# Seven half-size products instead of eight in the first product of the second layer's MLP

## The chip, the cores and the metric

The kernel runs on one core of a Trainium2 chip. The metric is the device time of one execution in microseconds. The engines of the core are called here as in the profile: PE (TensorE, the matrix engine, with PEld for its weight loads), DVE (VectorE), ACT (ScalarE), POOL (GpSimd) and SP (SyncE, which issues the DMAs).

## What is computed

One inference step of a trunk of two layers over 128 context tokens and 512 latent tokens (640 in all), model width 1024. Layer 0 mixes tokens with gated and retention scans, layer 1 with latent attention. After each mixer comes the part that this change is about:

```
def sq_relu_mlp(h, w1, w2):
    u = jax.nn.relu(jnp.einsum('bld,df->blf', h, w1))       # 1024 -> 4096
    return jnp.einsum('blf,fd->bld', jnp.square(u), w2)     # 4096 -> 1024

hc = pre_norm_mod(xc, norm_mlp_pre[l], sh2c, sc2c)          # context tokens; hl: latent tokens
xc = post_norm_residual(xc, sq_relu_mlp(hc, w_mlp1[l], w_mlp2[l]), norm_mlp_post[l], gt2c)
```

The shifts, scales and gates (sh2c, sc2c, gt2c) come from a product of a condition vector with w_ada, here called the modulation.

## The kernel before

All data are float32. A float32 product is made by PE from float32r operands: each operand is split into a rounded high part and a low part (the rest), and `mm3` issues three matmuls: high by high, high by low, low by high.

**Who sets the order.** Nothing is issued in the order of the source text. The parts of the computation are generators; a planner (`Weave`) runs them against its own cost table for each engine, and issues an instruction when its model says that the engine and the operands are there. On DVE, threads of a lower priority number come first, and among equals the one born first. Each engine then executes its instructions in the order so found; semaphores keep the data right. Since one helper (line 269) records every instruction, the profile shows that line for nearly all of them, and the tiles' names tell them apart. Buffers are handed out by `Slots`: `take` waits until one is free, `drop` gives it back.

**Weights.** `weights` loads each unit (512 KB, 128 partitions x 1024 elements) into one of 3 raw buffers. `weight_rooms` then takes room for high and low part from 10 slots of 4 KB per partition (`wp`), in the order of the list of units, and `weight_split` makes the high part on ACT (`wh`, a cast) and the low part on DVE (`wl`, a subtraction); then the raw buffer is given back. A unit holds two of the ten slots.

**The MLP** (`mlp`, called for each layer). The hidden width of 4096 is cut into 8 blocks of 512. The tokens after the norm lie transposed in `hT[0]` (high) and `hT[1]` (low), 128 rows of the width x 5 token tiles x 8 chunks x 128 tokens. In each block:
- The first product (`mlp1`) makes the hidden columns in four slices of 128 (f = 0 to 3), each for two groups of token tiles (three tiles, 384 tokens, and two tiles, 256). One product sums over 8 chunks of the width, 24 matmuls; a slice has 48. It takes a PSUM bank (`p1`) from `psg`, which has 3.
- `relu` takes the bank: ACT makes relu into `r` and its square into `hid` (high part), POOL squares `r` in place, DVE subtracts to get the low part.
- The second product (`mlp2`): for both halves of the 1024 output columns and the five token tiles, 4 slices x 3 matmuls of 512 columns into a bank `p2`; `add` adds the bank to `y` in SBUF (ACT copies it in block 0). In the last block the order is token tile by token tile, and `tail` makes the gated norm, the residual with `x` and the output.

A block needs 8 weight units: four for the first product, then four for the second (two for each output half).

**The modulation.** `ada_half` and `ada_cols` compute one section of it on DVE from tiles `rada` (256 KB loads), at a lower priority than the rest. In the second layer's MLP this is the last section, whose gate `tail` needs at the end; it starts in block 0, when `running` is set. Its sums lie in two buffers of their own (`pada`). `tmp` is a set of 4 temporaries that also others take.

Of the kernel before, what the change touches and what calls it, by code (L numbers as in the profile page):

```python
# [11 lines left out]
F32 = mybir.dt.float32  # L12
F32R = mybir.dt.float32r
# [6 lines left out]
P = 128  # L20
# [311 lines left out]
class Trunk:  # L332
# [70 lines left out]
    def weight(self, src, shape, lo="vector", pair=False, quota=None, room=None, prio=1):  # L403
# [2 lines left out]
        self.wlist.append((src, shape, ev, lo, pair, quota, room, prio))  # L406
        return ev

    def weights(self):

        loads = [Event() for _ in self.wlist]
        self.w.spawn(self.weight_rooms(loads))
        for item, load in zip(self.wlist, loads):
            if isinstance(item, Event):
                continue
            src, shape = item[:2]
            raw, hr = yield from self.take(self.raw, [P] + shape, F32, "raw")
            parts = list(src(raw) if callable(src) else [(raw, src)])
            self.w.aside(lambda: [self.nc.sync.dma_start(a, b) for a, b in parts],
                         then=lambda at: self.w.set(load, (raw, hr, at)))  # L420
            yield

    def weight_rooms(self, loads):
        for item, load in zip(self.wlist, loads):
            if isinstance(item, Event):
                yield item
                continue
# [153 lines left out]
    def ada_half(self, l, sec, half, rest, n=KC):  # L581

        nc = self.nc
        acc = [self.pada.tile([P, 512], F32, tag=f"ada{c}", name=self.nm("ada")) for c in range(2)]
# [12 lines left out]
        return acc  # L597

    def ada_cols(self, l, sec, half, acc, res, room=None):

        nc = self.nc
        tr, ht = room or (yield from self.take(self.tmp, [P, 512], F32, "tr"))
# [5 lines left out]
        self.drop(ht)  # L608
        yield
        ps, hp = yield from self.take(self.psg if room else self.psum, [P, 512], F32, "pc")  # L610
# [14 lines left out]
    def ada(self, l, sec, ev, rest, free=None):  # L625


        nc = self.nc
        res = self.mod_tile(sec)
        for half in range(2):  # L630
            if (l, sec) in ADA_EVEN:
                yield from self.ada_tensor(l, sec, half, res)
                continue
            acc = yield from self.ada_half(l, sec, half, rest)
            yield from self.ada_cols(l, sec, half, acc, res)
# [12 lines left out]
        self.drop(hr)  # L648
        self.w.spawn(self.gate_rows(dram, ev, free))
# [210 lines left out]
    def mlp_units(self, l):  # L860
        w1 = self.io["w_mlp1"][l].rearrange("(k p) f -> p k f", p=P)
        w2 = self.io["w_mlp2"][l].rearrange("(f p) n -> p f n", p=P)
        res = []
        for b in range(FF // 512):
            lo = "vector"
            prio = 0 if b else 1
            u1 = [self.weight(w1[:, :, fc * P:(fc + 1) * P], [KC, P], lo, prio=prio) for fc in range(b * 4, b * 4 + 4)]
# [138 lines left out]

    def mlp(self, ph, l, ready, xs, gate, mods, gfree):
        nc, io, w = self.nc, self.io, self.w
        shid = self.slots(ph, f"hid{l}", 5)
        sr = self.slots(ph, f"relu{l}", 4)  # L1010
        NB = FF // 512
        self.pada = self.pool(ph, f"ada{l}", 1)
        self.ada_later(ADA_MLP if l == 0 else ADA_LAST, self.slots(ph, f"rada{l}", 4))
# [19 lines left out]
        def tail(t, ev):  # L1033

            c = 0 if t == 0 else 1
            y, sm = ys[t][0], sms[t][0]
            gr = yield gate
            for half in range(2):
                ps, hp = yield ev[half]
                s = slice(half * 512, half * 512 + 512)  # L1040
                nc.vector.tensor_add(y[:, s], y[:, s], ps)
                self.drop(hp)
                yield
                nc.scalar.activation(self.junk[:, 0:512], y[:, s], AF.Square, accum_out=sm[:, 4 + half:5 + half])
                yield
                nc.vector.tensor_mul(y[:, s], y[:, s], gr[c][:, s])
                yield
            if gfree:
                self.at_last(left, lambda: w.set(gfree))
            x = xs[t][0]  # L1050
            if mods is None:
                dst = io["y_prompt"][0] if t == 0 else io["y_sample"][0, (t - 1) * P:t * P, :]
                yield from self.residual(x, y, sm, dst)
            else:
                yield from self.residual(x, y, sm)
                yield from self.pre_norm(t, x, y, sm, mods, out_ready)
            self.drop(ys[t][1], sms[t][1])

        def add(ps, hp, t, half, b):
# [4 lines left out]
                nc.vector.tensor_add(yh, yh, ps)  # L1064
            self.drop(hp)
            yield

        for b in range(NB):
            u1, u2 = self.u_mlp[l][b]
# [25 lines left out]
            if b == 0:  # L1095
                order = [(f, 0) for f in range(4)] + [(f, 1) for f in range(4)]

            for f, g in order:
                yield from mlp1(f, g)

            def mlp2(half, t, ev=None):
                ps, hp = yield from self.take(self.psg, [P, 512], F32, "p2")
# [15 lines left out]
                    w.spawn(add(ps, hp, t, half, b))  # L1118

            if b == 0:  # L1120
                w.set(self.running[l])
# [13 lines left out]
        if mods:  # L1135
            yield self.mod[1, 4]
        return out_ready


    def rope(self, out, x, lt, t12, rtab):  # L1140
# [908 lines left out]
```

## Time and profile before

| | us |
|---|---|
| median of three runs | 1542.08 (1541.82 to 1544.7) |
| the profiled execution | 1542.66 |
| its span, first to last instruction | 1540.9 |
| PE busy in the span | 1495.1 (97%) |
| DVE busy | 962.6 (62%) |
| ACT busy | 636.6 (41%) |
| POOL busy | 165.4 (11%) |

The rows below come from the profiled execution. A matmul's duration in the trace overlaps its neighbours' durations, so the cost of one is the step from start to start in a stretch without gaps. In rows of the timeline, neighbouring instructions of one kind are merged, and x2 means two of them. The second layer's MLP runs from 1087 to the end, the first layer's from about 357 to 803.

### The profile page before, as it was taken

The page shows a single profiled execution, that of the slowest core. Times are in us where ns is not written, and L with a number is a line of the kernel's source. Part 1 is how long each engine was busy: PE and PEld are TensorE (multiplying, and loading weights), DVE is VectorE, ACT ScalarE, POOL GpSimd, SP SyncE. Part 2 cuts the span into 40 slices and gives each one's busy share as a digit, 9 for nine tenths or more (in the row PEclk, how much of TensorE's full clock was granted, in tenths as well). Part 3 has the DMA queues.
Part 4 walks back from the last instruction along what each step waited for, and adds up shares of the span by engine and source line. Part 5 has one row for each costly group of instructions (what it writes and reads, how often), then busy time and mean ns, then how long its engine had stood idle before and what let it go on. Part 6 is the DMA issues. An engine that isn't in the chain of part 4 may idle for free.

```text
span 1540.9 us, 22938 instructions
## 1 busy us (share of the span) xinstructions
PE 1495.1 (97%) x8731; PEld 1329.5 (86%) x8731; DVE 962.6 (62%) x1912; ACT 636.6 (41%) x1467; POOL 165.4 (11%) x181
## 2 busy tenths in 40 slices
PE   5999999999999999999997999999999999999997
PEld 2687888889899889889987899988989988998996
DVE  4464674766777877777778788886675333334336
ACT  3583533555423223223256476665532322322322
POOL 0000210001021012012100100000101201210210
PEclk8999999999999999999998999999999999999999
DMA  9546222233655444444325000032353222222211
GB/s 329 161 155 216 86 69 69 68 96 110 179 158 145 144 135 142 140 136 145 102 66 143 19 22 24 33 107 79 110 172 109 71 81 69 83 82 67 72 55 68
DMA packets 146733, 166.18 MB, mean 108 GB/s; under 512 B 11984, under 2 KB 92480, under 8 KB 146624
## 3 DMA queue, kind: packets, MB, share of 16 engines
q1 hardware_dynamic: 146624, 164.73, 35.1%
q8 instruction: 68, 1.11, 0.3%
q14 instruction: 41, 0.34, 0.1%
HBM read 158.73 MB, written 5.96 MB: 107 GB/s over the span
## 4 chain that ended last, share of the span: by engine, by line
PE 91%; DVE 4%; ACT 2%; DMA 2%; issue 1%; SPq 0%; DVEq 0%; ACTq 0%
PE p L269 56%; PE pg L269 19%; PE ps L269 13%; PE pqk L269 2%; DMA rada<-in_w_ada 1%; PE pv L269 1%; DVE y L269 1%; DVE sm L269 1%; ACT junk L269 1%; DVE x L269 1%; DMA raw<-in_w_in_even 0%; ACT h L269 0%; DVE rope L269 0%; ACT sm L269 0%; PE pc L269 0%
## 5 line engine op out<-in xcount | busy, mean ns | idle before, releaser
L269 PE MATMUL p<-hT,wh 128*128 128x256 f32 (+1 forms) x2048 | 446.7, 309 | 0.0
L269 PE MATMUL p<-wh,hid 128*128 128x512 f32 x1280 | 399.3, 390 | 0.0
L269 PEld LDWEIGHTS p<-hT,wh 128*128 128x128 f32 x2048 | 345.5, 189 | 1.3
L269 PE MATMUL p<-hT,wl 128*128 128x256 f32 (+1 forms) x1024 | 317.0, 310 | 0.0
L269 ACT CAST wh<-raw 128x1024 fp32r<-128x1024 f32 (+3 forms) x169 | 172.8, 1026 | 266.8 <-PE p L269 231.8
L269 PEld LDWEIGHTS p<-wh,hid 128*128 128x128 f32 x1280 | 240.2, 188 | 49.3
L269 DVE TENSOR_TENSOR wl<-raw,wh 128x1024 fp32r<-128x1024 f32 (+3 forms) x165 | 197.3, 1199 | 132.9 <-ACT wh L269 128.0
L269 PE MATMUL pg<-wh,hT 128*128 128x512 f32 (+3 forms) x840 | 264.7, 389 | 0.0
L269 PE MATMUL p<-wl,hid 128*128 128x512 f32 x640 | 249.6, 390 | 0.0
L269 POOL TENSOR_TENSOR r<-r 128x384 f32<-128x384 f32 (+1 forms) x128 | 133.0, 1039 | 1008.4 <-ACT hid L269 890.1
L269 PEld LDWEIGHTS p<-hT,wl 128*128 128x128 f32 x1024 | 193.9, 189 | 0.0
L269 PEld LDWEIGHTS pg<-wh,hT 128*128 128x128 f32 x840 | 155.0, 190 | 32.3 <-issue 9.2
L269 ACT ACTIVATE r<-p 128x384 f32<-128x384 f32 (+1 forms) x128 | 56.1, 438 | 269.8 <-PE p L269 269.8
L269 DVE TENSOR_TENSOR y<-y,p 128x512 f32<-128x512 f32 x140 | 95.9, 685 | 93.2 <-PE p L269 92.8
L269 DVE SCALAR_TENSOR_TENSOR ada<-rada,cT,ada 128x512 f32<-128x512 f32 x196 | 146.7, 782 | 0.0
L269 PE MATMUL pg<-wl,hT 128*128 128x512 f32 (+3 forms) x360 | 141.7, 394 | 0.0
L269 PEld LDWEIGHTS p<-wl,hid 128*128 128x128 f32 x640 | 120.2, 188 | 24.1
L269 DVE TENSOR_TENSOR hid<-r,hid 128x384 fp32r<-128x384 f32 (+1 forms) x128 | 62.5, 488 | 124.3 <-POOL r L269 124.2
L269 PEld LDWEIGHTS pg<-wl,hT 128*128 128x128 f32 x360 | 68.6, 191 | 11.9 <-issue 2.5
L269 ACT ACTIVATE hid<-r 128x384 fp32r<-128x384 f32 (+1 forms) x128 | 60.4, 472 | 2.3
L269 PE MATMUL ps<-kn,qn 128*128 128x320 f32 (+1 forms) x216 | 47.8, 311 | 0.9 <-DVE hT L269 0.4
L269 PE MATMUL ps<-pt,v 128*128 128x256 f32 (+1 forms) x264 | 43.5, 290 | 1.1 <-DVE pt L269 0.7
(255 smaller groups left out, 1777.1 us busy)
## 6 DMA issues: line engine op xcount, KB each, us to landing
raw<-in_w_mlp SPq DMA_DIRECT2D x128, 512.0 KB, 4.1
rada<-in_w_ada SPq DMA_DIRECT2D x160, 256.0 KB, 3.2
rada<-in_w_ada SPq DMA_DIRECT2D x16, 512.0 KB, 8.7
raw<-in_w_in_even SPq DMA_DIRECT2D x16, 512.0 KB, 4.7
x<-in_x_sample SPq DMA_DIRECT2D x8, 512.0 KB, 7.4
gate<-gate SPq DMA_DIRECT2D x8, 512.0 KB, 4.5
raw<-in_w_out_even SPq DMA_DIRECT2D x8, 512.0 KB, 4.9
raw<-in_w_out_odd SPq DMA_DIRECT2D x8, 512.0 KB, 3.8
```

The lines of the kernel that those rows point to most:

```text
L269: emit = lambda: real(*a, **k)
```

## The change

In blocks 2 to 7 of the second layer (`PLAIN` = 2), the first product of two slices of 128 hidden columns at once is made by the scheme of Strassen and Winograd. Rows (chunks 0 to 3 and 4 to 7 of the width), hidden columns (the two slices) and tokens (the two halves of 64 of every tile) are halved, and the 2 x 2 x 2 = 8 products of halves are replaced by 7 products of 4 chunks and 320 tokens, of which four use sums or differences of weight halves, and four use sums or differences of token halves. `combine` makes the four quarters of the result from the seven. The second product and its weights are as before.

- **Weights** (`weight_pair`, `pair_load`, `pair_rooms`): the two units of a pair are loaded into two raw buffers together. DVE makes four differences of 512 elements in `tmp`; seven high parts (ACT) and seven low parts (DVE) of 512 elements go to one slot each. The raw buffers are given back when all that read them are done.
- **Tokens** (`token_sums`): the three sums S0 to S2 are made once, from 3 additions and 3 more sums for each token tile, and split into high and low part. They need space: the `x` tiles of the residual are written to DRAM as soon as a tile's norm is done, and their five buffers hold most of the sums; a pool `sums` has the rest. S3 is made when block 1's first product has been issued, and overwrites the quarter of `hT` that is no longer read. Then also four PSUM banks pass from `psum` to `psg`, which has 7.
- **Results**: DVE takes the banks (`p7`), ACT the first; `square` makes relu and square in one DVE operation, the high part on ACT and the low part on DVE. POOL has no part in it.
- **The loop**: the fourteen products of a block, then the second product, of which the first four banks are begun with slices 0 and 1, and continued with 2 and 3 afterwards. In the last block `load_back` loads `x` again once its last first product is issued.
- **The modulation** starts at block 3 in place of 0, has two buffers for its loads in place of four, and its sums lie in two of the four `tmp`.

```
+    def pair_rooms(self, got, at, evs):
+        (r0, h0), (r1, h1) = got
+        b11, b21, b12, b22 = r0[:, 0:4], r0[:, 4:8], r1[:, 0:4], r1[:, 4:8]
...
+        go(0, b11, (yield from room()), seen)
+        go(1, b21, (yield from room()), seen)
+        r = yield from room()
+        t1, ht1 = yield from tmp()
+        t2, ht2 = yield from tmp()
+        nc.vector.tensor_sub(t1, b12, b11)
+        nc.vector.tensor_sub(t2, b22, t1)
+        yield
...
+        nc.vector.tensor_sub(t3, b22, b12)
...
+        nc.vector.tensor_sub(t4, b21, t2)
...
+        go(6, b22, (yield from room()), seen)
...
     def mlp(self, ph, l, ready, xs, gate, mods, gfree):
+        seven = l == 1
-        sr = self.slots(ph, f"relu{l}", 4)
+        sr = self.slots(ph, f"relu{l}", 7 if seven else 4)
-        self.pada = self.pool(ph, f"ada{l}", 1)
+        self.pada = None if seven else self.pool(ph, f"ada{l}", 1)
...
+            if seven:
+                xs[t] = yield xev[t]
...
+        def square(r, hr, h, half, ev):
+            s = slice(half * 64, half * 64 + 64)
+            rv = r.rearrange("p (t q) -> p t q", q=64)
+            nc.vector.scalar_tensor_tensor(r, r, 0.0, r, op0=ALU.max, op1=ALU.mult)
+            yield
+            nc.scalar.copy(h[:, 0, :, s], rv)
+            yield
+            nc.vector.tensor_sub(h[:, 1, :, s], rv, h[:, 0, :, s].bitcast(F32))
...
+        def products(units, hid, hev):
+            A = [[[self.hT[i][:, :, k + j, q:q + 64] for j in range(4)] for i in range(2)]
+                 for k, q in ((0, 0), (4, 0), (4, 64))]
...
+            for i, tok in enumerate((A[0], A[1], S[1], S[0], S[2], A[2], S[3])):
+                if i == 2:
+                    yield three
+                if i == 6:
+                    yield four
+                wh, wl, held = yield units[i]
+                ps, hp = yield from self.take(self.psg, [P, 512], F32, "p7")
+                for k in range(4):
+                    self.mm3(ps[:, 0:320], wh[:, k], wl[:, k], tok[0][k], tok[1][k], k == 0, k == 3)
+                self.drop(*held)
+                w.set(done[i], (ps[:, 0:320], hp))
+                yield "next"
...
+            if seven and b >= PLAIN:
+                if b == PLAIN + 1:
+                    w.set(self.running[l])
...
+                def begin(i):
+                    banks[i] = yield from self.take(self.psg, [P, 512], F32, "p2")
+                    yield from part2(*todo[i], (0, 1), banks[i][0])
+                pair = [products(u1[i], hid, hev) for i in range(2)]
+                for p in (0,) * 7 + (1,) * 7:
+                    yield from step(pair[p])
+                if last:
+                    self.drop(*xtokens)
+                    w.spawn(load_back())
...
+                for i, (half, t) in enumerate(todo):
+                    while len(banks) < min(len(todo), i + (4 if i == 0 else 1)):
+                        yield from begin(len(banks))
+                    yield from part2(half, t, (2, 3), ps)
...
+    def token_sums(self, S, rest, ready, xs, parked, tokens, sr, first_done, three, four):
+        for t in range(NT):
+            yield ready[t]
+            nc.sync.dma_start(parked[t], xs[t][0])
+            self.drop(xs[t][1])
...
+            nc.vector.tensor_add(a11, h(0, t, 0, 0), h(1, t, 0, 0))
+            nc.vector.tensor_add(a21, h(0, t, 0, 64), h(1, t, 0, 64))
+            nc.vector.tensor_add(s1, h(0, t, 4, 64), h(1, t, 4, 64))
+            nc.vector.tensor_add(s1, s1, a21)
+            nc.vector.tensor_sub(s2, s1, a11)
+            nc.vector.tensor_sub(a11, a11, a21)
...
+PLAIN = 2
```

`combine` has, for each pair, one ACT copy of a bank and seven DVE sums of 320 elements that read a bank, and four calls of `square`.

## Rows read from the trace of the kernel before

**Rows 1.** The page, busy time by engine and the chain by engine.

```profile
PE 1495.1 (97%) x8731; PEld 1329.5 (86%) x8731; DVE 962.6 (62%) x1912; ACT 636.6 (41%) x1467; POOL 165.4 (11%) x181
...
PE 91%; DVE 4%; ACT 2%; DMA 2%; issue 1%; SPq 0%; DVEq 0%; ACTq 0%
```

**Rows 2.** Chain in order of time, second MLP: start us, us, engine and tile.

```profile
1173.10 340.48 PE p L269 x1908
```

**Rows 3.** PE timeline, block 0 of that MLP: start us, us, operation, shape, count.

```profile
1095.70 0.51 PE L269 MATMUL p<-hT,wh 128*128 128x384 f32 x2
...
1100.38 0.51 PE L269 MATMUL p<-hT,wh 128*128 128x384 f32 x2
...
1105.45 0.40 PE L269 MATMUL p<-hT,wh 128*128 128x256 f32 x2
...
1116.96 0.40 PE L269 MATMUL p<-wh,hid 128*128 128x512 f32 x1
...
1118.12 0.62 PE L269 MATMUL p<-wh,hid 128*128 128x512 f32 x2
...
1131.04 0.62 PE L269 MATMUL p<-wh,hid 128*128 128x512 f32 x2
```

**Rows 4.** The same, first matmul of the second product in block 2.

```profile
1228.32 0.40 PE L269 MATMUL p<-wh,hid 128*128 128x512 f32 x1
```

**Rows 5.** PE timeline, second layer's input projection: 320 columns.

```profile
854.01 1.92 PE L269 MATMUL pg<-wh,hT 128*128 128x320 f32 x12
855.77 0.90 PE L269 MATMUL pg<-wp,hT 128*128 128x320 f32 x5
```

**Rows 6.** Busy us by engine, granted clock, DMA: blocks 0 and 3 (second MLP).

```profile
1087.00:1144.00 57.00, 57.00 (x329) 52.19 (x328) 38.56 (x70) 28.38 (x60) 6.71 (x8) 1.00 0.42 125
...
1255.00:1310.60 55.60, 55.60 (x315) 50.87 (x314) 20.16 (x26) 15.05 (x25) 8.66 (x8) 1.00 0.26 76
```

**Rows 7.** The same view, a block of the first layer's MLP.

```profile
526.20:581.60 55.40, 55.40 (x315) 50.55 (x314) 43.84 (x66) 15.43 (x33) 8.65 (x8) 1.00 0.49 143
```

**Rows 8.** DVE groups by form: count, busy us, mean ns (ada: second MLP alone).

```profile
L269 DVE TENSOR_TENSOR wl<-raw,wh 128x1024 fp32r<-128x1024 f32 x153 | 186.8, 1223 | 122.9 <-ACT wh L269 122.6
...
L269 DVE TENSOR_TENSOR y<-y,p 128x512 f32<-128x512 f32 x140 | 95.9, 685 | 93.2 <-PE p L269 92.8
...
L269 DVE TENSOR_TENSOR hid<-r,hid 128x384 fp32r<-128x384 f32 x64 | 35.7, 557 | 100.8 <-POOL r L269 100.8
...
L269 DVE TENSOR_TENSOR hid<-r,hid 128x256 fp32r<-128x256 f32 x64 | 26.8, 419 | 23.5 <-POOL r L269 23.5
...
L269 DVE TENSOR_TENSOR wp<-raw,wp 128x512 fp32r<-128x512 f32 x16 | 10.9, 685 | 1.8 <-ACT wp L269 1.6
...
L269 DVE SCALAR_TENSOR_TENSOR ql<-pg,sm,qpe 128x256 f32<-128x256 f32 x5 | 2.4, 482 | 0.1
...
L269 DVE SCALAR_TENSOR_TENSOR ada<-rada,cT,ada 128x512 f32<-128x512 f32 x28 | 20.7, 781 | 0.0
```

**Rows 9.** ACT group by form: the cast of half a weight.

```profile
L269 ACT CAST wp<-raw 128x512 fp32r<-128x512 f32 x16 | 9.9, 624 | 1.8 <-PE p L269 1.8
```

**Rows 10.** MLP weight loads (KB, median us to landing); landings between 1187 and 1320.

```profile
raw<-in_w_mlp SPq DMA_DIRECT2D x128, 512.0 KB, 4.1
...
DMA to landing us min/median/max: 4.0/4.1/5.1
```

**Rows 11.** Busy us by engine and granted clock, end of the first MLP.

```profile
810.00:815.00 5.00, 1.40 (x12) 1.18 (x11) 4.63 (x12) 4.14 (x14) 0.00 (x0) 1.00 0.22 42
...
815.00:820.00 5.00, 2.18 (x9) 1.89 (x9) 5.00 (x15) 2.23 (x7) 0.00 (x0) 0.50 0.78 273
```

**Rows 12.** The end: busy by window, PE's last matmul, the chain's last residual.

```profile
1520.00:1525.00 5.00, 5.00 (x24) 4.14 (x23) 4.08 (x9) 1.59 (x6) 0.00 (x0) 1.00 0.28 105
...
1532.22 0.39 PE L269 MATMUL p<-wh,hid 128*128 128x512 f32 x1
...
1536.58 0.75 DVE x L269
```

**Rows 13.** DMA issues: `x` written to DRAM in the attention, KB, us to landing.

```profile
park<-x SPq DMA_DIRECT2D x5, 512.0 KB, 4.1
```

More of the change, by code (lines that the diff above doesn't have):

```diff
@@ L407, in weight, with weight_pair, pair_load, done @@
         return ev
+    def weight_pair(self, w1, fc):
+        evs = [Event() for _ in range(7)]
+        self.wlist.append((w1, fc, evs))
+        return evs
+    def pair_load(self, w1, fc, load):
+        got = []
+        for i in range(2):
+            got.append((yield from self.take(self.raw, [P, KC, P], F32, "raw")))
+        at = [0.0]
+        left = [2]
+        def done(t):
+            at[0] = max(at[0], t)
+            left[0] -= 1
+            if not left[0]:
+                self.w.set(load, (got, at[0]))
+        for i in range(2):
+            self.w.aside(lambda i=i: self.nc.sync.dma_start(got[i][0], w1[:, :, (fc + i) * P:(fc + i + 1) * P]), then=done)
+            yield
@@ L414, in weights @@
             if isinstance(item, Event):
+                continue
+            if len(item) == 3:
+                yield from self.pair_load(item[0], item[1], load)
                 continue
@@ L426, in weight_rooms @@
                 yield item
+                continue
+            if len(item) == 3:
+                got, at = yield load
+                yield from self.pair_rooms(got, at, item[2])
                 continue
@@ L583, in ada_half @@
         nc = self.nc
-        acc = [self.pada.tile([P, 512], F32, tag=f"ada{c}", name=self.nm("ada")) for c in range(2)]
+        acc, held2 = [], []
+        for c in range(2):
+            if self.pada:
+                acc.append(self.pada.tile([P, 512], F32, tag=f"ada{c}", name=self.nm("ada")))
+            else:
+                a, ha = yield from self.take(self.tmp, [P, 512], F32, "ada")
+                acc.append(a)
+                held2.append(ha)
         for kc in range(n):
@@ L596, in ada_half, with ada_cols @@
             yield rest
-        return acc
-    def ada_cols(self, l, sec, half, acc, res, room=None):
+        return acc, held2
+    def ada_cols(self, l, sec, half, acc, held, res):
         nc = self.nc
-        tr, ht = room or (yield from self.take(self.tmp, [P, 512], F32, "tr"))
+        tr, ht = yield from self.take(self.tmp, [P, 512], F32, "tr")
         sm, hs = yield from self.take(self.rows, [P, 2, 16], F32, "sums")
@@ L607, in ada_cols @@
             yield
-        self.drop(ht)
+        self.drop(ht, *held)
         yield
-        ps, hp = yield from self.take(self.psg if room else self.psum, [P, 512], F32, "pc")
+        ps, hp = yield from self.bank()
         nc.tensor.matmul(ps[:, 0:32], self.fold, sm.rearrange("p c b -> p (c b)"), start=True, stop=True)
@@ new lines, in combine @@
+        def combine(done, first, second):
+            (ha, ea), (hb, eb) = first, second
+            keep = lambda: self.take(sr, [P, 320], F32, "c")
+            p, hp = yield done[0]
+            u, hu = yield from keep()
+            nc.scalar.copy(u, p)
+            self.drop(hp)
+            p, hp = yield done[1]
+            c, hc = yield from keep()
+            nc.vector.tensor_add(c, u, p)
+            self.drop(hp)
+            w.spawn(square(c, hc, ha, 0, ea[0]))
+            yield
+            p, hp = yield done[2]
+            nc.vector.tensor_add(u, u, p)
+            self.drop(hp)
+            p5, hp5 = yield done[3]
+            c12, hc12 = yield from keep()
+            nc.vector.tensor_add(c12, u, p5)
+            yield
+            p, hp = yield done[4]
+            nc.vector.tensor_add(u, u, p)
+            self.drop(hp)
+            c, hc = yield from keep()
+            nc.vector.tensor_add(c, u, p5)
+            self.drop(hp5)
+            w.spawn(square(c, hc, hb, 1, eb[1]))
+            yield
+            p, hp = yield done[5]
+            nc.vector.tensor_add(u, u, p)
+            self.drop(hp)
+            w.spawn(square(u, hu, ha, 1, ea[1]))
+            yield
+            p, hp = yield done[6]
+            nc.vector.tensor_add(c12, c12, p)
+            self.drop(hp)
+            w.spawn(square(c12, hc12, hb, 0, eb[0]))
@@ L1068, in mlp, with step @@
+        def step(gen):
+            value = None
+            while True:
+                try:
+                    y = gen.send(value)
+                except StopIteration:
+                    return
+                if isinstance(y, str):
+                    return
+                value = yield y
         for b in range(NB):
@@ L1096, in mlp, with part2 @@
                 order = [(f, 0) for f in range(4)] + [(f, 1) for f in range(4)]
+            def part2(half, t, fs, ps):
+                for f in fs:
+                    if uw[half][f // 2] is None:
+                        uw[half][f // 2] = yield u2[half][f // 2]
+                    for ev in hev[f]:
+                        yield ev
+                    wh, wl, held = uw[half][f // 2]
+                    self.mm3(ps, hid[f][0][:, 0, t], hid[f][0][:, 1, t], wh[:, f % 2], wl[:, f % 2], f == 0, f == 3)
+                    uses[half][f // 2] -= 1
+                    hid_uses[f] -= 1
+                    if not uses[half][f // 2]:
+                        self.drop(*held)
+                    if not hid_uses[f]:
+                        self.drop(hid[f][1])
+                yield
@@ L1098, in mlp @@
             for f, g in order:
                 yield from mlp1(f, g)
+            if seven and b == PLAIN - 1:
+                w.set(first_done)
             def mlp2(half, t, ev=None):
@@ L1120, in mlp @@
             if b == 0:
-                w.set(self.running[l])
+                if not seven:
+                    w.set(self.running[l])
                 for t in range(NT):
```

126 lines of the change are left out of this document (122 added, 4 removed).

## The prediction

> **What bounds the kernel now.** I read the busy shares and the chain by engine first [rows 1]: TensorE is busy 97% of the span and carries 91% of the chain that ended last. Then the chain in order of time across the second layer's MLP [rows 2]: one unbroken piece of TensorE's products, 340.48 us long, with nobody to wait for. Then the engines' busy time by block [rows 6]: TensorE fills the whole stretch at a granted clock of 1.00 (2.4 GHz), while VectorE has 20.16 of 55.6 us and ScalarE 15.05. So in this stage a matmul column taken away is time taken away, as long as the other engines keep TensorE fed.
>
> The profiled execution took 1542.66 us (span 1540.9); the median of the runs shown is 1542.08, 0.58 below it. The sum is made against 1542.66, and 0.58 comes off at the end. About 0.2% (3 us) is what a measurement of this kernel can tell from no change.
>
> **What a matmul costs.** Steps between starts, not the durations, since matmuls overlap. In [rows 3] 27 matmuls of 384 columns take 1100.38 - 1095.70 = 4.68, 0.1733 us each; 96 of 256 take 1116.96 - 1105.45 = 11.51, 0.1199; 57 of 512 take 12.92, 0.2267. The three lie on one line: 0.0133 us plus 0.417 ns a column. At 320 it gives 0.1467, and 12 matmuls of 320 in the second layer's input projection take 1.76 us, 0.1467 each [rows 5].
>
> **The first product.** Per pair of 128-column blocks it has now 2 x 8 x 3 = 48 matmuls of 384 and 48 of 256: 48 x (0.1733 + 0.1199) = 14.07 us. After: 7 products x 4 chunks x 3 = 84 of 320: 84 x 0.1467 = 12.32. Saved 1.75 per pair, 3.5 per block, in six blocks (2 to 7): **21.0 us**. A block shrinks from 2 x 14.07 + 120 x 0.2267 = 55.4 (the second product of block 2 starts 1228.32 - 1116.96 = 2 x 55.7 after that of block 0 [rows 3, 4]) to 24.6 + 27.2 = 51.8. All of it is on the path [rows 2].
>
> The Trainium skill has another price: "TensorE: Matmul & The Clock Gate", section "Back-to-back issue gap", gives N/2.4 + 2.5 ns for a warm matmul, so a fixed part of 2.5 and not the 13.3 ns that rows 3 show; by it the pair would go from 13.0 to 11.4 us, an estimate of 19.6 us saved. The rows differ from the page, and they decide.
>
> Four of the seven products (A0, A1, A2, S3: 48 of the 84 matmuls) read tokens in runs of 64 columns instead of 128; no row shows such a run. Runs of 128 (the 384 and 256 forms) lie on the line of the contiguous 512 [rows 3], so a break costs 0 to perhaps 0.003 us a matmul, 0 to 1.7 us in 576. I take 0, the value of the nearest rows. A bank change: the first five matmuls of the second product took 1118.12 - 1116.96 = 1.16 instead of 1.13 [rows 3], 0.03 lost. Products go from 8 to 14 a block, each with a weight unit and a bank to wait for: 6 x 6 x 0.03 = **+1.0 us** (0 to 3).
>
> **VectorE and ScalarE, beside the path.** Per pair: 4 differences and 7 low parts of 512 elements at 0.685 (form of wp), 7.5 us; 7 sums out of PSUM, 4 squares and 4 low parts of 320, priced between 0.419 (hid, 256) and 0.557 (hid, 384), for the squares from 0.482 (ql, 256): about 0.5 each, 7.5 [rows 8]. Two pairs 30.0; four second weights at 1.223, 4.9; ten additions at 0.685, 6.9: 41.8 of 51.8 us, where 20.16 is now [rows 6]. The nearest stretch is in the first layer's MLP: VectorE busy 43.84 of 55.4 and TensorE 55.40, nothing lost [rows 7]. So 0 is taken; 81% there against 79% is why this is no certainty. ScalarE: 14 casts of 512 at 0.624 [rows 9], 8.7, four of 1024 and ten copies of 320: some 18 of 51.8. GpSimd's squares go away there.
>
> **The weights of the second pair** are the tightest chain. A pair holds two of three raw buffers until its last unit is split. There are 10 rooms; counted in the order of their use, a block's seventh is one that the second product before it gives back after the last use of its third weight unit, six matmuls of 512 or 1.4 us before its end. From there: cast 0.62, low part 0.69, and the next pair's two loads can be issued at about 0 of the new block. Landing 4.1, at most 5.1 us after issue [rows 10], two of them by about 6.5; first unit ready at about 8. TensorE wants it at 12.3. The seventh is wanted at 22.9; VectorE must by then do 7.5 us of weights beside 7.5 of combining, from 6.5 on some 15: ready by about 20 to 21.5. Cover 4 and 1.5 to 3 us. If it is gone, TensorE waits by the excess in each of six blocks. The second product's second weight unit, loaded when those raw buffers come free (about 20, landed 25, split 27.5), is wanted at 24.6 + 5.4 = 30, because four banks are begun with the first half of the hidden blocks. The same 5.4 us cover the last combine chain (addition, square, cast, low part: some 2.2 us plus waits). I take 0.
>
> **Moved and added elsewhere.** The last modulation's 28 + 4 products (20.7 us and some 7 of sums [rows 8]) leave blocks 0 and 1 and come from block 3 on; at 10 us spare a block they need three to four blocks, and the gate is wanted only after block 7 begins its second product, over 200 us later. Its products are ahead of the second weights where both wait, and hold two of the four temporaries: 0 to 3 us in each of blocks 3 to 5. The token sums (some 95 VectorE operations of at most 0.42 us, 32 us in all) take the place that the modulation leaves in blocks 0 and 1, where VectorE was busy 38.56 of 57 with it [rows 6]; the first part is wanted in block 2, 60 us after its start, the second 10 us into block 2. Their danger is a low part of block 0's hidden delayed behind them; the first is wanted at 1116.96. I take 0 (0 to 4).
>
> SP's queue gets five writes of 512 KB at the start, 4.1 us each [rows 13], and five loads back when the last first product ends; a row for a load's landing back is missing, so 4.1 to 8 for each. Behind the writes stand weight loads that are not urgent; the residual of the first tile wants its x 8 us and more after the loads are issued. **The tail:** TensorE's last matmul starts at 1532.22, the last residual at 1536.58, VectorE is busy 4.08 of 5 us [rows 12]. The first token tile gets its two halves 2.7 us later than now (four banks begun together), the last at the same point: 0 to 2, taken **+0.5**.
>
> **Sum:** 1542.66 - 21.0 + 1.0 + 0.5 = 1523.2; against the median 1522.6.
>
> **The rivals.**
> - *The feed runs a little short.* The raw buffers or VectorE's queue make TensorE wait 1 to 3 us in each of six blocks: 1528 to 1541, 1534 in the middle. For: 81% on VectorE, the 1.5 to 3 us of cover, the modulation in blocks 3 to 5. Against: rows 7.
> - *Slower: the products are bound by VectorE.* If no unit of a pair is prepared under the second product (rooms or raw buffers handed on too late), both pairs' 30 us of weights and combining stand under 24.6 us of products, with 1.2 for a second weight unit: 6.6 us lost a block, 40 in six, less 19.5 gained: about 1562. It decides from 3.3 us of waiting per block on. Long waits cost more than themselves: where TensorE was busy 1.40 and then 2.18 of 5 us, the granted clock fell from 1.00 to 0.50 [rows 11]. The Trainium skill ("TensorE: Matmul & The Clock Gate", Part 1) says the same, that the clock is gated unless the array is kept busy; the trace agrees with 0.50. For: one pair's weights need 7 of 10 rooms and two of three raw buffers. Against: six rooms come free half a second product, 13.6 us, before the block.
> - *Nothing gained.* A matmul of 320 columns might be held by its weight load, as many loads as matmuls; rows 3 and 5 speak against it, since 256 columns step at 0.1199. It would take a step of 0.1675 for 320: 1542.
>
> **How the numbers follow.** Forecast 0.64 (1519 to 1527); feed a little short 0.20 (1528 to 1541, most of it below 1536); slower 0.11 (1547 to 1580); nothing gained 0.05. Low end: all small costs at 0, 1521, and two below it for the line's error; high end 1536, where under 2 in 10 is left out. Faster by over 0.2% (below 1539): 0.64 and 0.19 of the 0.20, 0.83; within 0.2%: 0.05 and the other 0.01, 0.06; slower 0.11.
>
> **What would show it.** Right: the step of a 320-column product is 0.147 and a block from 2 on is 51.8 us; the chain stays TensorE's from block 2 to 7 without a piece of VectorE; VectorE is busy about 38 to 42 us a block; the granted clock stays 1.00. Wrong: idle time of TensorE before a p7 matmul, ended by VectorE or ScalarE (weights), or by a load of raw; a step above 0.150 in the four products with runs of 64; blocks 3 to 5 longer than 6 and 7 (modulation); a clock below 1.00 in any of them; x loaded back after its residual is due.

## The result, and the profile after

| | before | changed |
|---|---|---|
| executions, us | 1541.82, 1542.08, 1543.48, 1544.70 | 1522.98, 1524.25, 1525.28 |
| ratio of the times, 95% interval | | 0.9878 (0.9858 to 0.9897) |
| profiled execution, us | 1542.66 | 1522.98 |
| its span, us | 1540.9 | 1521.2 |
| from the start of the second MLP (the first matmul of its first product) to the end, us | 453.94 | 434.03 |

A fourth execution of the changed kernel, at a mean clock of 0.65, is left out; with it the median of the four would be 1524.76. The change takes 1.2% off. The spans differ by 19.7 us; the second MLP alone is 19.9 shorter, and starts 0.2 later.

The page of the changed kernel: busy us by engine, the chain by engine, and the group of the new products that read `hT` (the others read the sums).

```profile
PE 1473.8 (97%) x8587; PEld 1308.4 (86%) x8587; DVE 1092.6 (72%) x2247; ACT 651.7 (43%) x1526; POOL 113.0 (7%) x133
...
PE 89%; DVE 4%; ACT 3%; DMA 2%; issue 1%; SPq 0%; DVEq 0%; ACTq 0%
...
L269 PE MATMUL p<-hT,wq 128*128 128x320 f32 x576 | 88.1, 310 | 0.0
```

Against [rows 1]: PE's share of the span is the same 97% of a shorter span, VectorE has 130 us more, GpSimd 52 less. The chain in order of time (start us, us, engine and tile) in the second MLP is still PE's alone, as in [rows 2]; it is cut at three places, which are the modulation's small products on PE (at 1304.4, 1357.1 and 1359.3), and the waits view of PE has no line between 1087 and the end, so the cuts are no idle time.

```profile
1102.51 202.03 PE p L269 x1129
1304.68 52.52 PE p L269 x292
...
1359.62 131.97 PE p L269 x752
```

PE's timeline in block 2 (start us, us, operation, tiles, shape, count) shows the new products, first of the two pairs, and then the second product's first matmul:

```profile
1199.78 3.68 PE L269 MATMUL p<-hT,wq 128*128 128x320 f32 x24
1203.29 1.48 PE L269 MATMUL p<-s,wq 128*128 128x320 f32 x9
...
1208.57 7.20 PE L269 MATMUL p<-hT,wq 128*128 128x320 f32 x48
1215.61 1.48 PE L269 MATMUL p<-s,wq 128*128 128x320 f32 x9
...
1224.41 0.39 PE L269 MATMUL p<-wh,hid 128*128 128x512 f32 x1
```

The starts carry the case. 24 matmuls with runs of 64 columns take 1203.29 - 1199.78 = 3.51, 0.1463 each; 48 take 7.04, 0.1467 each. All 168 take 24.63; before, block 2's first product took 28.15 (1200.17 to the 1228.32 of [rows 4]). The stretch from that 1224.41 to the next block at 1251.64 is 27.23, as before (1228.32 to 1255.55).

Busy us by engine (PE, PEld, DVE, ACT, POOL), granted clock, DMA share and GB/s: the blocks 0 to 6 of the changed kernel, then block 6's first products and its second product apart.

```profile
1087.20:1144.40 57.20, 57.20 (x330) 52.36 (x328) 36.93 (x89) 32.27 (x78) 6.04 (x8) 1.00 0.34 111
1144.40:1199.80 55.40, 55.40 (x314) 50.71 (x313) 36.05 (x84) 18.59 (x42) 8.07 (x8) 1.00 0.19 58
1199.80:1251.60 51.80, 51.80 (x289) 47.16 (x288) 37.98 (x66) 16.13 (x28) 0.00 (x0) 1.00 0.28 82
1251.60:1303.50 51.90, 51.90 (x290) 47.18 (x289) 49.36 (x85) 16.02 (x28) 0.00 (x0) 1.00 0.39 112
1303.50:1355.60 52.10, 52.10 (x292) 47.41 (x291) 49.55 (x89) 16.53 (x32) 0.00 (x0) 1.00 0.43 122
1355.60:1408.10 52.50, 52.50 (x293) 47.40 (x292) 38.97 (x70) 17.01 (x33) 0.00 (x0) 1.00 0.33 101
1408.10:1459.90 51.80, 51.80 (x289) 47.15 (x288) 37.97 (x66) 16.13 (x28) 0.00 (x0) 1.00 0.28 82
1408.10:1432.70 24.60, 24.60 (x169) 24.60 (x168) 22.75 (x41) 11.08 (x19) 0.00 (x0) 1.00 0.42 124
1432.70:1459.90 27.20, 27.20 (x122) 22.55 (x121) 15.22 (x26) 5.05 (x10) 0.00 (x0) 1.00 0.15 44
```

PE is busy in every microsecond, at 1.00. VectorE is at 73% of a block without the modulation and at 95% in the two with it (3 and 4); the last two lines show where the 73% lie: 92% of the first products, 56% of the second product.

### The profile page after: what moved, and what is told of

It is laid out like the page before. It is cut to its first block, busy times and chain, and to the rows that moved or that the text cites. A ratio compares the mean times of both kernels' runs of the same rounds, so it can differ in the third digit from the quotient of the medians.

```text
span 1521.2 us, 22996 instructions
## 1 busy us (share of the span) xinstructions
PE 1473.8 (97%) x8587; PEld 1308.4 (86%) x8587; DVE 1092.6 (72%) x2247; ACT 651.7 (43%) x1526; POOL 113.0 (7%) x133
## 4 chain that ended last, share of the span: by engine, by line
PE 89%; DVE 4%; ACT 3%; DMA 2%; issue 1%; SPq 0%; DVEq 0%; ACTq 0%
PE p L269 55%; PE pg L269 19%; PE ps L269 13%; PE pqk L269 2%; DVE y L269 1%; PE pv L269 1%; ACT junk L269 1%; DVE sm L269 1%; DMA raw<-in_w_in_even 1%; DVE x L269 1%; DMA x<-in_x_sample 1%; DMA raw<-in_w_out_odd 1%; ACT h L269 0%; SPq L269 0%; DVE rope L269 0%
## 5 line engine op out<-in xcount | busy, mean ns | idle before, releaser
L269 PE MATMUL p<-hT,wh 128*128 128x256 f32 (+1 forms) x1280 | 280.1, 310 | 0.0
L269 DVE TENSOR_TENSOR wl<-raw,wh 128x1024 fp32r<-128x1024 f32 (+3 forms) x141 | 167.9, 1195 | 73.8 <-ACT wh L269 73.4
L269 PEld LDWEIGHTS p<-hT,wh 128*128 128x128 f32 x1280 | 216.1, 190 | 0.8
L269 ACT CAST wh<-raw 128x1024 fp32r<-128x1024 f32 (+3 forms) x145 | 147.6, 1022 | 137.9 <-PE p L269 98.6
L269 PE MATMUL p<-hT,wl 128*128 128x256 f32 (+1 forms) x640 | 198.7, 310 | 0.0
L269 POOL TENSOR_TENSOR r<-r 128x384 f32<-128x384 f32 (+1 forms) x80 | 80.6, 1007 | 729.1 <-ACT hid L269 392.8
L269 PEld LDWEIGHTS p<-hT,wl 128*128 128x128 f32 x640 | 121.3, 190 | 0.0
L269 PE MATMUL p<-hT,wq 128*128 128x320 f32 x576 | 88.1, 310 | 0.0
L269 PEld LDWEIGHTS p<-hT,wq 128*128 128x128 f32 x576 | 85.5, 188 | 0.5
L269 ACT CAST wq<-tw 128x512 fp32r<-128x512 f32 x48 | 27.6, 618 | 71.0 <-DVE tw L269 61.7
```

The source lines that it names most:

```text
L269: emit = lambda: real(*a, **k)
```

## The experiments

Each ran beside the kernel before on the same chip; ratios are to that. The start of the second MLP varies between executions (1084.96 to 1089.60 where no edit reaches it), so where a us counts, the time from that start to the end is compared: 453.94 before, 434.03 changed.

**1. The changed kernel again**, without an edit.

> The changed kernel once more, as the yardstick for the others. Theory (TensorE's path: 84 matmuls of 320 in place of 48 of 384 and 48 of 256, all else covered): 1523 to 1525, 0.987 to 0.989 of before; blocks 2, 3 and 6 at 51.9 us.

1523.01 us, ratio 0.9867 (0.9851 to 0.9884); 434.01 from the start of the MLP to the end. The gain stands.

**2. Four blocks in place of six.** The modulation stays at block 3.

```
-PLAIN = 2
+PLAIN = 4
```

> Seven products in blocks 4 to 7 alone (PLAIN = 4), the modulation still from block 3. Theory of the path: the gain is 3.5 us for each converted block, so two fewer give back 7: 1530.5 to 1532. Rival (the gain comes from what is done once: seven PSUM banks, the modulation moved, the second product begun in four banks): within 1 us of the changed kernel, 1523 to 1525. Rival (the feed takes back part in each block): less than 7 is given back.

1529.29, 0.991 (0.9895 to 0.9925). From start to end 441.1: 7.1 us more than six blocks, 3.55 a block. The gain goes block by block with the products, and PE waits nowhere.

**3. Everything that is done once, without the products.** The sums S0 to S2 are made and not read, S3 is left out, `x` is written and loaded back, the banks pass over, the modulation starts at block 3; all eight blocks compute as before.

```
-PLAIN = 2
+PLAIN = 8
...
-            if seven and b == PLAIN - 1:
-                w.set(first_done)
...
             if b == NB - 1:
+                if seven:
+                    self.drop(*xtokens)
+                    w.spawn(load_back())
```

> Everything that the change does once, without the seven products: all eight blocks as in the kernel before (PLAIN = 8), with the token sums S0 to S2 made and not read, x written out and loaded back, seven PSUM banks, the modulation from block 3. S3 is left out, since it would overwrite tokens that are still read. Theory of the path: none of these is on the path, so 1541 to 1544, 0.998 to 1.001 of before, and every block stays at 55.4. Rival (the gain comes from these parts): 1523 to 1535.

1543.89, 1.0008 (0.9999 to 1.0018); blocks of 55.4, and 55.8 where the modulation's small products lie; 454.8 from start to end, 0.9 more than before, 0.7 of it after the last block's second product begins. So the once-only parts give nothing and cost about that much, at the end.

**4. Seven blocks in place of six, in three orders.** One plain block is left as cover for the token sums.

```
-PLAIN = 2
+PLAIN = 1
```

> Seven products in blocks 1 to 7 (PLAIN = 1, the modulation from block 2). Theory that only the path counts: 3.5 us less, 1520 to 1521.5. Rival, from the trace of the changed kernel: the sums of tokens end at 1158.4 there, block 1 starts at 1144.4 and wants them for its third product at 1147.9, so TensorE waits some 10 us, and the last sum (22.9 us from its first to its last operation there) is wanted 7 us after the third product: another 10 to 16 us of waiting, and time at the lower clock. That gives 1537 to 1550. I hold the rival for right.

1540.96, 0.9984 (0.9974 to 0.9993): another block converted, and nearly the whole gain gone. Block 1 took 72.0 us in place of 51.86. PE's waits in the second MLP (who, for what: us in total, times, longest), and the window of the worst of it with the columns as above:

```profile
PE p L269 <- ACT hT L269: 9.6, 1, 9.6
PE p L269 <- ACT s L269: 2.7, 1, 2.7
PE p L269 <- DVE s L269: 2.6, 1, 2.6
```

```profile
1165.00:1170.00 5.00, 0.00 (x0) 0.00 (x0) 4.14 (x16) 0.69 (x2) 0.00 (x0) 0.78 0.34 105
1170.00:1175.00 5.00, 2.59 (x9) 2.42 (x10) 2.15 (x8) 0.53 (x2) 0.00 (x0) 0.50 0.00 0
```

`s` and `hT` are the token sums, not weights. 14.9 of the 20.2 us lost are waits; after 5 us without a matmul the granted clock is 0.50 (1.2 GHz), and slower products are what is left for the rest. If the sums' place in VectorE's order is all that is wrong, moving them ahead mends it:

```
-            w.spawn(self.token_sums(...))
+            w.spawn(self.token_sums(...), None, -1)
```

> As e3, and the thread of the token sums has priority -1 in place of 0, so that on VectorE and ScalarE its operations go before the others where both are ready. VectorE's work for the sums is some 32 us, from 1108 on. If the 50 us that they took in the changed kernel were waiting behind other work, they end at about 1135 (first part) and 1150 (last sum), before block 1 wants them (1147.9 and 1155): 3.5 us less than the changed kernel, 1520 to 1521.5, block 1 at 51.9. Rival: they are held by their own chain between VectorE and ScalarE and not by the queue, and TensorE waits in block 1: 1530 to 1545. Second rival: block 0's hidden parts come late behind them, a wait of TensorE before block 0's second product.

1530.34, 0.9919 (0.9904 to 0.9933). S0 to S2 came in time, S3 did not; block 1 took 61.5 us, with this one long wait:

```profile
PE p L269 <- ACT hT L269: 6.2, 1, 6.2
```

So the product that reads S3 was put last, in both pairs, with the same priority of the sums:

```
-                for p in (0,) * 7 + (1,) * 7:
+                for p in ((0,) * 6 + (1,) * 6 + (0, 1) if b == PLAIN else (0,) * 7 + (1,) * 7):
```

> As e4 (seven products from block 1, the token sums before the other work), and in block 1 both pairs' seventh products, which read S3, come after the other twelve. In e4 TensorE waited 6.2 us for S3, which came some 17 us after block 1's start and was wanted 10.6 after it. Now it is wanted 21.1 us after the start. Theory: the wait is gone, the combine chain after the two late products costs 0 to 2 us, block 1 takes 52 to 54 us, and from the MLP's start to the end it takes 431 to 433 us against 434.0 of the changed kernel: 1520 to 1523. Rival (S3 needs what the first products' combining takes from VectorE, and comes as much later): 1526 to 1531 as in e4.

1530.61, 0.9912 (0.9898 to 0.9927); block 1 again 61.6 us. No product waits for S3 now, but PE waits 4.5 us for `hid` and 2.5 for `wq`, and the windows of block 1 show VectorE full from 1155 on:

```profile
1155.00:1165.00 10.00, 7.46 (x47) 6.67 (x47) 9.90 (x32) 3.23 (x7) 0.00 (x0) 1.00 0.16 52
1165.00:1175.00 10.00, 8.84 (x59) 8.36 (x57) 10.00 (x19) 3.97 (x5) 0.00 (x0) 1.00 0.35 111
```

Both orders missed what the theory expected of them, and neither beats six blocks: the sums and a converted block's own work do not fit into VectorE together. Two plain blocks are the cover of the sums. In the changed kernel the sums' first and last operations (VectorE by tile: count, duration ns, first and last start) lie so:

```profile
L269 DVE TENSOR_TENSOR s<-hT,hT x20: 418/420/429, 1108.4 to 1190.3; 128x256 f32<-128x256 f32 x20
L269 DVE TENSOR_TENSOR sums<-s,sums x15: 211/220/227, 1116.5 to 1158.4; 128x64 fp32r<-128x64 f32 x15
...
L269 DVE TENSOR_TENSOR hT<-s,hT x5: 419/421/429, 1177.2 to 1195.1; 128x256 fp32r<-128x256 f32 x5
```

S0 to S2 take from 1108.4 to 1158.6, 50 us, and are wanted at 1203.3; S3 is done at 1195.5 and wanted at 1210.3.

**5. Fewer raw buffers, and fewer rooms.** One of the three raw buffers, and in another kernel two of the ten rooms, are taken at the first pair and never given back.

```
     def pair_load(self, w1, fc, load):
+        if not hasattr(self, "kept"):
+            self.kept = yield from self.take(self.raw, [P, KC, P], F32, "raw")
```

> One of the three raw buffers is taken away from the first pair on. The second product's four weight units can then be loaded only after the second pair's raw buffers are given back. By the prediction's chain: those come free at about 17 to 20 of a block, the first unit lands at 21.5 to 24.5 and is split at 24 to 27, wanted at 24.6; the second is wanted at 30. Theory (cover of the weights is a few us): TensorE waits 0 to 2.5 us a block, 1523 to 1538. Rival (the raw buffers are handed on so early that there is much more cover): 1522 to 1525. Rival (each block waits a whole load, 4 us and more): 1548 and more.

```
     def pair_rooms(self, got, at, evs):
+        if not hasattr(self, "kept"):
+            self.kept = yield from self.take2(self.wp, [P, 2, 4, P], F32R, "wq")
```

> Two of the ten slots for split weights are taken away from the first pair on. By the prediction's count a pair's last two units then get their rooms at the end of the second product before and just after it. In the changed kernel the second pair's units were all ready 12.5 us after the block's start, wanted from 12.3 to 22.9 on. Theory (cover of some 6 to 10 us): 0 to 1 us lost a block, 1522 to 1527. Rival (rooms are the tight chain, as the prediction has it with 4 and 1.5 to 3 us of cover): 2 to 4 us lost in each of six blocks, 1535 to 1548.

1523.26, 0.9872 (0.9855 to 0.9888), and 1524.65, 0.9876 (0.9859 to 0.9892); from start to end 434.4 in the second, and PE waits nowhere in either. Neither buffer is short in the changed kernel. With two raw buffers the second product's first weight unit was ready at 1428.8 and wanted at 1433.66, 4.9 us of cover left.

**6. More work for VectorE.** Each pair of slices gets n more subtractions of 272 elements on a tile that nobody reads, about 0.35 us each: n = 14 (10 us a block), 28 (20 us), 6 (4 us).

```
+        def burn():
+            o = self.wide.rearrange("p k c -> p (k c)")
+            for _ in range(14):
+                nc.vector.tensor_sub(o, o, o)
+                yield
...
             done = [Event() for _ in range(7)]
+            w.spawn(burn())
```

> The changed kernel with 14 more VectorE operations of 272 elements per pair of hidden slices (in place on a buffer that is no longer needed; some 0.37 us each, 10 us a block). VectorE was busy 38.0 of 51.8 us in blocks 2, 5 and 6, and 49.5 in 3 and 4 with the modulation. Theory: TensorE waits for VectorE only when VectorE's sum reaches the block's length: 48.4 of 51.8 without the modulation, so TensorE keeps 51.9 to 52.5 a block and the modulation is spread over more blocks: 1523 to 1530. Rival (the cover of the second pair's weights, 1.5 to 4 us by my prediction, is what decides): 10 us more in a block eat it, TensorE waits 3 us or more in each of six blocks: 1540 and more.

1572.25, 1.02 (1.0181 to 1.0219): slower than the kernel before. The 1523 to 1530 of a VectorE with 10 us to spare was wrong. Two of its blocks, 2 and 6 (columns as above), and PE's three largest waits:

```profile
1199.30:1254.80 55.50, 52.69 (x289) 46.89 (x288) 46.92 (x94) 16.42 (x28) 0.00 (x0) 1.00 0.26 76
1439.40:1503.90 64.50, 55.28 (x293) 49.87 (x292) 51.53 (x100) 17.12 (x33) 0.00 (x0) 0.92 0.28 82
```

```profile
PE p L269 <- DVE wq L269: 18.4, 8, 3.4
PE ps L269 <- DVE sums L269: 7.8, 1, 7.8
PE p L269 <- ACT hid L269: 3.6, 2, 2.6
```

VectorE is busy 85% of block 2 and 80% of block 6, and PE waits for it in both: in the changed kernel 95% cost nothing. So the share of a block does not decide it. Two things show in the trace. First, the work is wanted early: 22.75 of 24.6 us of the first products are VectorE's already, so nearly all of the 10 us is pushed behind them, where it delays the second slices' hidden columns (block 2 has the 2.6 us for `hid`). Second, the modulation: the waits for `wq` lie in blocks 3 to 5, beside it. VectorE's timeline in block 6, where the last of it runs:

```profile
1457.80 3.29 DVE L269 TENSOR_TENSOR wide<-wide 128x272 f32<-128x272 f32 x7
1461.00 0.68 DVE L269 TENSOR_REDUCE sums<-tr 128x16 f32<-128x512 f32 x1
...
1462.46 0.69 DVE L269 TENSOR_REDUCE sums<-tr 128x16 f32<-128x512 f32 x1
1463.07 0.68 DVE L269 TENSOR_TENSOR tw<-raw,raw 128x512 f32<-128x512 f32 x1
```

The pair's difference `tw`, urgent work, follows right behind the modulation's last reduction. The modulation holds three of the four temporaries at that point, and at its low priority it gets to run last: the urgent work waits for the buffers of work that is held back. PE's small product `ps<-sums,fold` stands at the head of its queue all the while (the 7.8 us above). The second pair's first two units, which need no temporary, were ready 7.7 and 9.4 us into the block, the third, which does, at 26.6. In blocks 4 and 5 the raw buffers have a part too. Both loads of block 4's second pair were issued only at its start (1311.28 and 1311.80; 3 us before it in the changed kernel), its first unit was ready 14.9 us into the block, wanted at 12.3, and the chain that ended last (start us, us) goes through the load:

```profile
1309.47 1.42 DVE ada L269 x2
1311.80 6.60 DMA raw<-in_w_mlp
```

> The same with 28 operations per pair, some 20.7 us a block: VectorE would need 58.7 us in a block of 51.8. Theory: now VectorE bounds the blocks, each takes 58 to 60 us, the modulation's 28 us come on top of them, TensorE idles with VectorE as its releaser, and the granted clock falls below 1.00 where the waits are long: 1565 to 1600, slower than before. Rival (VectorE's operations are not what feeds TensorE): 1523 to 1530.

One execution: 1640.0, mean clock 0.955 (0.987 before); waits for `wq` 40.9 us, for `hid` 21.5 on ACT, for `sums` 20.5; blocks 2 to 6 of 64.5 to 78.7 us. As expected in kind, VectorE is the bound; in size it is beyond the 1565 to 1600.

To tell the modulation's part from the rest, the 10 us were kept and the modulation was put back to block 0:

```
+                w.set(self.running[l])      # at block 0
-                if b == PLAIN + 1:
-                    w.set(self.running[l])
```

> As e6 (14 operations more per pair), and the modulation starts in block 0 as in the kernel before, so that it is done before the seven products begin. In e6 block 2, with no modulation beside it, took 55.5 us, and blocks 4 to 6 64, their first products 36 to 37 in place of 24.6. Theory A (in e6 the modulation, starved on VectorE, keeps two and three of the four temporaries that the next pair's differences need): without it every block takes what block 2 took, 54 to 57, and the whole 1536 to 1550. Theory B (VectorE's sum alone): 28 us fewer in six blocks, but each block that has VectorE full stays at 60 and more: 1560 to 1575.

1559.96, 1.01 (1.0085 to 1.0115). The blocks 3 to 6, now without it, took 55.5 to 57.2 us, against 56.6, 64.3, 63.7 and 64.5 above; so the modulation, its work and the buffers that it holds together, is worth 6.5 to 9 us in each of the blocks 4 to 6. The total is not what the account with 54 to 57 a block gives, since the modulation now competes with the token sums and ends only in block 2, which took 64.5. Block 4 in its two halves:

```profile
1323.10:1347.80 24.70, 24.70 (x170) 24.68 (x169) 24.41 (x55) 10.13 (x17) 0.00 (x0) 1.00 0.28 86
1347.80:1380.30 32.50, 29.66 (x122) 23.43 (x121) 22.60 (x40) 6.18 (x13) 0.00 (x0) 0.95 0.22 65
```

The first products lose nothing, VectorE is at 99% of them, and the loss (32.5 for 27.2) comes in the second product; of PE's 22 us of waits in this kernel 11.7 are for `hid`.

> 6 operations more per pair, some 4.4 us a block, the modulation from block 3 as in the changed kernel. VectorE was busy 22.75 of the 24.6 us of the first products in block 6 of the changed kernel and 15.22 of the 27.2 us of its second. Theory (what decides is VectorE's work while the first products run, and a part of it can slip 5 us into the second product): 27.1 us of work, blocks 2, 6 and 7 keep 52 to 53, blocks with the modulation lose 0 to 4 each: 1523 to 1535. Rival (any added work is waited for): 4.4 a block, 1548 and more. Rival (the whole block's sum decides): nothing lost but in the modulation's blocks, 1523 to 1526.

1533.08, 0.9929 (0.9914 to 0.9943), with these blocks 2 to 6:

```profile
1200.20:1252.00 51.80, 51.80 (x289) 47.13 (x288) 41.45 (x78) 16.23 (x28) 0.00 (x0) 1.00 0.28 82
1252.00:1303.90 51.90, 51.90 (x290) 47.17 (x289) 49.86 (x92) 16.18 (x28) 0.00 (x0) 1.00 0.33 92
1303.90:1361.70 57.80, 53.72 (x291) 47.15 (x290) 48.56 (x94) 16.56 (x32) 0.00 (x0) 1.00 0.32 92
1361.70:1417.70 56.00, 54.01 (x289) 48.20 (x289) 49.48 (x92) 16.05 (x28) 0.00 (x0) 0.97 0.38 113
1417.70:1470.10 52.40, 52.40 (x293) 47.39 (x292) 42.57 (x82) 16.74 (x33) 0.00 (x0) 1.00 0.33 101
```

4 us cost nothing in a block without the modulation, and 5.8 and 3.5 us in two of the three with it (the third, block 3, is the one in which it starts). The changed kernel stands that near to losing.

## Why the prediction was right

1522.6 was forecast; the changed kernel took 1522.98 to 1525.28, and 1523.01 in experiment 1. Of the spans' 19.7 us, by starts of blocks (before against changed): start of the MLP +0.21; blocks 0 and 1 -0.60; from block 2's start to the last second product's start 305.05 and 284.80, -20.25; from there to the end 35.68 and 36.62, +0.94. The forecast's sum was -19.5.

- **The step of 320 columns and the 21.0 us.** Right: 0.1467, and 28.15 - 24.63 = 3.52 a block, 21.1 in six; experiment 2 has 3.55. The Trainium skill ("TensorE: Matmul & The Clock Gate", "Back-to-back issue gap") has a fixed part of 2.5 ns for an isolated warm matmul, by which the estimate was 19.6; the measured step keeps to the 13.3 ns of [rows 3].
- **Runs of 64 columns.** Right at 0: 0.1463 and 0.1467, the same as the contiguous sums.
- **Bank changes, +1.0.** Mis-sized: 168 x 0.1467 = 24.64, and 24.63 were measured. Fourteen products a block in place of eight cost nothing.
- **The tail, +0.5.** It was +0.94. The last residual comes 31.72 after the last second product's start, 31.36 before: 0.36. Experiment 3, whose last block is as before, has 31.36 too, so it comes with the new last block; the order with four banks begun together would explain it (no run tried that apart). The other 0.58 lies behind the last residual (4.90 for 4.32), nearly all of it between the issue of the last output write and the end of SyncE's waits for it (2.67 for 2.11). Experiment 3, without the seven products, has 5.04 there, so the parts done once may be its cause; with a single profile of the kernel before, that is not shown.
- **A term left out: PE's own share of the modulation.** Its few small matmuls moved from blocks 0 and 1 (-0.60) to blocks 4 and 5, which last 52.08 and 52.50 in place of 51.86 (+0.86), +0.26 in all. With the 0.44 that the tail took beyond its 0.5 it makes good 0.70 of the 1.0 that the banks did not cost: the sum came out as near as it did partly by luck, because small errors met.
- **VectorE beside the path, 0.** Right in its result, wrong in its reason. 41.8 us a block were forecast, 37.97 measured. The sum used durations, and on a full VectorE these overlap as PE's do. The timeline of block 6 shows it: two operations of 512 elements take 1.29 us as a pair, 0.69 alone, and one of 320 (0.49) is followed 0.40 later by the next:

```profile
1415.32 0.49 DVE L269 TENSOR_TENSOR c<-c,p 128x320 f32<-128x320 f32 x1
1415.72 1.29 DVE L269 TENSOR_TENSOR wq<-tw,wq 128x512 fp32r<-128x512 f32 x2
...
1419.28 0.69 DVE L269 TENSOR_TENSOR wq<-tw,wq 128x512 fp32r<-128x512 f32 x1
1419.88 0.69 DVE L269 TENSOR_TENSOR wq<-raw,wq 128x512 fp32r<-128x512 f32 x1
1420.60 0.49 DVE L269 TENSOR_TENSOR c<-c,p 128x320 f32<-128x320 f32 x1
```

  The Trainium skill ("Vector Engine (DVE) Microarchitecture Reference", section 5.2) gives 1.0417 ns a column and about 75 ns an instruction for a stream of them: 0.61 us for 512 and 0.41 for 320. The trace agrees (0.60 and 0.40), and by it the block's 32 operations of 512, 30 of 320 and 4 of 1024 come to 36.3, an estimate nearer to the 37.97 than 41.8 was. But the share of a block, against which [rows 7] was held, isn't the measure at all (experiment 6): what counts is the first products' 24.6 us, where VectorE has 1.9 to spare, and the 5.4 us that the second product's early start on the first slices lends.
- **The second pair's weights, 0.** Right in its result, wrong in its chain. The forecast let both loads wait for the first pair's last unit, and go out at the new block's start. Counted in the list's order, they were issued at 1379.71 and 1397.25, 28 and 11 us before block 6; the load at its start (1408.07) is already that of the second product's first unit, and the pair's first difference, which reads both raw buffers, starts at 1408.89. The first pair's first raw buffer was free again once its fourth difference was made (1397.18). So the pair's first unit was ready 6.6 us into block 6, wanted at 12.3; its last low part, the last line but one of the fence, ends at 1420.57, 12.5 us into the block, wanted at 22.9. 5.7 and 10.4 us of cover, not 4 and 1.5 to 3; in block 4, with the modulation, 3.1 and 5.2. With one raw buffer fewer (experiment 5) the last unit of block 6 was ready at the same 12.5, with two rooms fewer at 15.4. The forecast also let the weights queue behind all of the combining at the price of durations; in the trace they alternate with it.
- **Token sums, 0.** Right only because of the two plain blocks: 32 us of operations take 50 and, for S3, 23 us from first to last, and with one plain block they cost 10 to 20 us (experiment 4).
- **The modulation, 0 to 3 us in blocks 3 to 5.** It needed two blocks, not three to four, and PE waited in neither. Its grip on the temporaries, which the forecast named, shows in experiment 6 with 10 us more of work. With 4 us more its blocks lose time too, but there block 4's second pair is also loaded late (1303.83 and 1304.31, at the block's start), and no run gave the modulation buffers of its own.
- **x loaded back.** Two writes whose landing the trace has took 6.2 and 6.9 us, not the 4.1 of [rows 13]; they have the whole MLP. Three of the loads back took 6.8 to 9.2, where 4.1 to 8 was forecast. The last was issued at 1480.8 and landed at 1489.7, and the first residual starts at 1497.9.

**The rivals.** *Nothing gained* fell with the step. *The feed a little short* fell: no wait of PE. *Slower, bound by VectorE* did not happen, but the mechanism is there: experiment 6 turns the gain into 30 us of loss with 10 us of VectorE work a block. Without the modulation it comes from the first products' stretch; beside it, from the temporaries, and in two blocks also from raw buffers handed on late, as the rival had it. That each long wait also costs clock, as it said from [rows 11], showed in experiment 4: 0.50 behind 5 us without a matmul.

Open: what lengthens the last 0.58 us; and the split of the modulation's part, with 10 us more of work, between its own operations, the temporaries and the raw buffers, which was read from the waits and the chain and not tried apart.

## What to carry to other kernels

Matmuls traded for VectorE work are worth their steps in full only while VectorE has room in the stretch that waits for that work; look there, not at the share of a block or of the span. Price a full VectorE by steps from start to start, as PE, and keep a stretch of unconverted work as cover for what is made once. Where low-priority work takes buffers from a set that urgent work uses, it can stop the urgent work while it is itself held back (block 6 of experiment 6).

## What the runs showed of the hardware that was not expected

- A moving operand read in runs of 64 columns of float32 costs nothing: 0.1463 to 0.1467 us for 320 columns, as for contiguous ones.
- PE passes from one PSUM bank to the next, and from block to block, without a gap: 168 matmuls in 24.63 us.
- The same part of a program starts up to 4.6 us apart in different executions (1084.96 to 1089.60 for the second MLP). A difference of 1 us has to be read from starts within the stage.
